# Weight sums of the block products: VectorE subtractions replaced by accumulating DMA transfers

## Chip, cores and metric

One core of one Trainium2 chip runs the whole program in one launch. The metric is device microseconds of one execution, the median of several runs; lower is better.

## What is computed

A trunk of two encoder layers on 512 tokens of width 1024, in float32, with a last RMSNorm. Each layer is

```python
x = x + 0.5 * swiglu(rmsnorm(x, ffn1_norm), ffn1_wg, ffn1_wu, ffn1_wd)
x = x + concat[neighbourhood attention, gated linear attention](rmsnorm(x, mix_norm)) @ w_out
x = x + 0.5 * swiglu(rmsnorm(x, ffn2_norm), ffn2_wg, ffn2_wu, ffn2_wd)

def swiglu(h, w_gate, w_up, w_down):
    return (jax.nn.silu(h @ w_gate) * (h @ w_up)) @ w_down
```

The change touches the gate and up projections (`h @ w_gate`, `h @ w_up`, 1024 by 2816) of the four feed-forward passes.

## The kernel before

Activations are held transposed, features in the partitions and tokens along the free axis, and all matrix products are made to float32 accuracy from a high and a low part: `split` makes the high part on ScalarE (ACT, line 149) and the remainder on VectorE (DVE, line 150), and `mm3` issues three matmuls (lines 176 to 178): high by high, high by low, low by high.

**Block products.** A pass has 11 column blocks of 256 for the gate and 11 for the up projection. The first three of each are computed directly (`direct_pairs`). The other eight pairs, 16 blocks a pass and 64 in all, go through `smat`, which replaces eight half-size partial products by seven, in the manner of Strassen and Winograd. Of the weights it takes four quarters a21, a11, a12, a22, each a 128 by 512 part of one tile `wraw`, loaded by one 1024 KB transfer on SyncE's queue (line 157), and four sums of them, s1 to s4. The activations' sums t1 to t4 are made once a pass in `prep_pair`. A partial product (`prod`) is 12 matmuls of 256 columns. In the order in which TensorE (PE) does them, the seven are: a12, a22, a11, s1, then s3 of the block before (`flush`, which runs the deferred `last`), then s2 and s4.

**Buffers.** `wraw` has two buffers, and the down projection's weights go through the same two. The split parts `wh` and `wl` have six each, for seven splits a block. So a split waits until a partial product ahead has given its buffer back, and the splits of one block run while TensorE still works on the block before. The four sums are tiles of their own (tag `ws`, five buffers), so `wraw` is free again once a12, a22 and a11 are split and the sums taken.

**Order.** Each engine works through a fixed list, written by the framework's scheduler, which lays the instructions out in time by its own estimates. An instruction that waits holds up all behind it in its engine's list. Between the feed-forward blocks lie the down projections: with `GROUPS = (4, 4, 3)` and three direct pairs, a pass has 3 block products, a down projection, 8 block products, a down projection, 5 block products, and the last down projection.

GpSimd (POOL) issues only the 32 loads of the attention bias (line 874).

Of the kernel before, what the change touches and what calls it, by code (L numbers as in the profile page):

```python
# [9 lines left out]
F32 = mybir.dt.float32  # L10
F32R = mybir.dt.float32r
U8 = mybir.dt.uint8
AF = mybir.ActivationFunctionType
ALU = mybir.AluOpType

P = 128
T = 512
H2 = T // 2
# [45 lines left out]
def trunk_kernel(ctx, tc, xin, wgu, wdn, win, wcode, wgate, wout, vec, rpbt,  # L64
                 lmask, onesid, out, depth=DEPTH, stop=None):
    nc = tc.nc
    V, S, G, PE = nc.vector, nc.scalar, nc.gpsimd, nc.tensor
# [18 lines left out]
    def gvec(stage, c):  # L86
        return vecs[:, stage * KD + c: stage * KD + c + 1]
# [12 lines left out]
    def nm(s):  # L100
        cnt[0] += 1
        return f"{st['lab']}_{s}_{cnt[0]}"

    def sl(name="s", dt=F32, tag="sl"):
        return sp.tile([P, T], dt, tag=tag, name=nm(name), bufs=TAGS[tag])
# [11 lines left out]
    def psum(tag):  # L117
        pool = {"mm": pm, "sc": ps2}.get(tag, ps1)
        return pool.tile([P, T], F32, tag=tag, name=nm(tag))
# [27 lines left out]
    def split(src, h, l, gain=None):  # L147
        if gain is None:
            S.activation(h, src, AF.Copy)  # L149
            V.tensor_tensor(l, src, h.bitcast(F32), op=ALU.subtract)  # L150
        else:
            S.activation(h, src, AF.Copy, scale=gain)
            V.scalar_tensor_tensor(l, src, gain, h.bitcast(F32), ALU.mult, ALU.subtract)

    def wload(src, n):
        raw = wp.tile([P, 2048], F32, tag="wraw", name=nm("wraw"))
        nc.sync.dma_start(raw[:, :n], src)
        return raw

    def wnew():  # L160
        return [wp.tile([P, T], F32R, tag=t, name=nm(t), bufs=6) for t in ("wh", "wl")]

    def wsplit(src, n=T):
        h, l = wnew()
        split(src, h[:, :n], l[:, :n])
        return h, l
# [8 lines left out]
    def mm3(ps, wh, wl, rh, rl, first, last, more=False):  # L175
        PE.matmul(ps, wh, rh, start=first, stop=False, skip_group_check=more)  # L176
        PE.matmul(ps, wh, rl, start=False, stop=False, skip_group_check=more)  # L177
        PE.matmul(ps, wl, rh, start=False, stop=last, skip_group_check=more)  # L178
# [6 lines left out]
    def prep_pair(i, stage):  # L185
        s = st["s"]
        ya, yb = sl("y"), sl("y")
        V.scalar_tensor_tensor(ya, xt[:, 2 * i, :], gvec(stage, 2 * i), s, ALU.mult, ALU.mult)
        V.scalar_tensor_tensor(yb, xt[:, 2 * i + 1, :], gvec(stage, 2 * i + 1), s, ALU.mult, ALU.mult)
        ta, tb = sl("y"), sl("y")  # L190
        b11, b12, b21, b22 = ya[:, :H2], ya[:, H2:], yb[:, :H2], yb[:, H2:]
        t1, t2, t3, t4 = ta[:, :H2], ta[:, H2:], tb[:, :H2], tb[:, H2:]
        V.tensor_tensor(t1, b12, b11, op=ALU.subtract)
        V.tensor_tensor(t2, b22, t1, op=ALU.subtract)
        V.tensor_tensor(t3, b22, b12, op=ALU.subtract)
        V.tensor_tensor(t4, b21, t2, op=ALU.subtract)
        tag = ("na", "na", "g0", "g1")[i]
        h0 = sl("xc", F32R, tag)
        split(b11, h0[:, :H2], h0[:, H2:])
        parts = [(h0[:, :H2], h0[:, H2:])]  # L200
        if i < 2:
            xg = gp_.tile([P, 4, T], F32R, tag="ga", name=nm("xc"))
        for j, src in enumerate((yb, ta, tb)):
            if i < 2 and j < 2:
                h, l = xg[:, 2 * j, :], xg[:, 2 * j + 1, :]
            else:
                h, l = sl("xc", F32R, tag), sl("xc", F32R, tag)
            split(src, h, l)
            parts += [(h[:, :H2], l[:, :H2]), (h[:, H2:], l[:, H2:])]
        XC[i] = dict(zip(("b11", "b21", "b22", "t1", "t2", "t3", "t4"), parts))  # L210
# [60 lines left out]
    def flush():  # L271
        while pend:
            pend.pop(0)()

    def wprep(src):
        raw = wload(src, 2048)
        a21, a11, a12, a22 = (raw[:, i * T:(i + 1) * T] for i in range(4))
        w12, w22, w11 = wsplit(a12), wsplit(a22), wsplit(a11)
        s1, s2, s3, s4 = (sl("ws", F32, "ws") for _ in range(4))
        V.tensor_tensor(s1, a21, a22, op=ALU.add)  # L280
        V.tensor_tensor(s2, s1, a11, op=ALU.subtract)
        V.tensor_tensor(s4, a12, s2, op=ALU.subtract)
        V.tensor_tensor(s3, a11, a21, op=ALU.subtract)
        return w12, w22, w11, wsplit(s1), s2, s4, s3

    def smat(src, post):
        w12, w22, w11, ws1, s2, s4, s3 = st.pop("pre", None) or wprep(src)
        o1, o2 = sl("o1"), sl("o2")

        def prod(ps, w, part, new=True):  # L290
            h, l = w
            for i in range(KP):
                c = slice(i * P, (i + 1) * P)
                mm3(ps, h[:, c], l[:, c], *XC[i][part], new and i == 0, i == KP - 1, not new)

        Y = psum("mm")
        Dp, Cp = Y[:, :H2], Y[:, H2:]
        prod(Dp, w12, "b21")
        yield
        prod(Cp, w22, "t4")  # L300
        S.activation(o1[:, :H2], Dp, AF.Copy)
        S.activation(o2[:, :H2], Cp, AF.Copy)
        yield
        A = psum("mm")[:, :H2]
        prod(A, w11, "b11")
        ws2, ws4, ws3 = wsplit(s2), wsplit(s4), wsplit(s3)
        V.tensor_tensor(o1[:, :H2], A, o1[:, :H2], op=ALU.add)
        yield
        B = psum("mm")[:, :H2]
        prod(B, ws1, "t1")  # L310
        S.activation(o2[:, H2:], B, AF.Copy)
        yield
        flush()
        yield
        prod(A, ws2, "t2", False)
        S.activation(o1[:, H2:], A, AF.Copy)
        yield
        prod(B, ws4, "b22", False)
        V.tensor_tensor(o1[:, H2:], B, o1[:, H2:], op=ALU.add)
        yield  # L320

        def last():
            prod(A, ws3, "t3", False)
            V.tensor_tensor(o2[:, H2:], A, o2[:, H2:], op=ALU.add)
            V.tensor_tensor(o2[:, :H2], A, o2[:, :H2], op=ALU.add)
            post(o1, o2)

        pend.append(last)

    def run(gen):  # L330
# [38 lines left out]
    def ffn(l, which):  # L369
# [9 lines left out]
        def gate_up(hid):  # L379
            n = fp[0]  # L380
            fp[0] += 1
            sg = []

            def post_g(o1, o2):
                for o in (o1, o2):
                    S.activation(o, o, AF.Silu)
                    sg.append(o)

            def post_u(o1, o2):
                for o, g in zip((o1, o2), sg):  # L390
                    V.tensor_tensor(o, o, g, op=ALU.mult)
                    add_hid(hid, o)

            yield from smat(wgu[idx, n, 0], post_g)
            yield from smat(wgu[idx, n, 1], post_u)

        def direct_pairs(hid):
# [25 lines left out]
            for i in range(3):  # L423
                prep_pair(i, stage)
            b11 = dmat(wgu[idx, 1, 1], ("tp", "o"))
            evac(b00, b01)
            prep_pair(3, stage)
            if NDF == 3:
                b20 = dmat(wgu[idx, 2, 0], ("mm", "mm"))
# [758 lines left out]
```

## Time and profile before

| | |
|---|---|
| median of 3 runs | 1929.98 us (1929.54 to 1930.05) |
| the profiled execution | 1929.63 us, of which the span is 1927.9 us |
| granted TensorE clock | 0.998 of full speed over the span |
| busy, share of the span | PE 99%, PEld 87%, DVE 73%, ACT 53%, POOL 1% |
| mean DMA rate | 97 GB/s |

PE is TensorE's matmuls, PEld its weight loads, which overlap them. Busy time is that of instructions at work, not of queues that wait. The span runs from the first to the last instruction; the time beside it holds what lies around them.

### The profile page before, as it was taken

The numbers are of one execution on the slowest core, as the hardware profiler recorded it, in microseconds if no ns is written. First come the engines' busy times: TensorE is split into PE (matmuls) and PEld (weight loads), VectorE is DVE, ScalarE is ACT, GpSimd is POOL, SyncE is SP. The second block draws the span as 40 slices with busy tenths as digits, with TensorE's granted clock in tenths as the row PEclk, the third lists the DMA queues.
The fourth block names the chain that finished last, engine by engine and source line by source line (L and its number), as shares of the span: only waits on it lengthen the run. The fifth ranks groups of instructions, "written<-read, shape, count | busy, mean of one in ns | idle before, by whom it ended". The sixth has DMA issues, their size and how long they took to land.

```text
span 1927.9 us, 32197 instructions
## 1 busy us (share of the span) xinstructions
PE 1912.1 (99%) x12490; PEld 1676.2 (87%) x12490; DVE 1412.6 (73%) x2705; ACT 1030.1 (53%) x1968; POOL 17.4 (1%) x36
## 2 busy tenths in 40 slices
PE   9999999999999999999999999999999999999997
PEld 8889989878788898989889899987887878999896
DVE  7958768677558976958787596776765688678585
ACT  6535536466665553635555264455666655446264
POOL 0000000000000000000000000000000000000000
PEclk9999999999999999999999999999999999999999
DMA  5332323322113322332323233232221133323322
GB/s 178 108 107 97 99 99 128 111 78 83 56 42 112 105 96 102 110 110 83 112 91 101 96 110 110 88 121 96 98 91 37 44 118 109 110 88 110 109 78 77
DMA packets 58249, 187.78 MB, mean 97 GB/s; under 512 B 6640, under 2 KB 13296, under 8 KB 45808
## 3 DMA queue, kind: packets, MB, share of 16 engines
q1 hardware_dynamic: 30480, 133.12, 20.3%
q10 hardware_dynamic: 25056, 44.22, 6.9%
q0 software_dynamic: 2560, 8.39, 1.3%
q8 instruction: 98, 1.61, 0.4%
q14 instruction: 55, 0.45, 0.1%
HBM read 183.60 MB, written 2.10 MB: 96 GB/s over the span
## 4 chain that ended last, share of the span: by engine, by line
PE 98%; DVE 1%; DMA 1%; ACT 0%; issue 0%; DVEq 0%; ACTq 0%
PE F_mm L176 14%; PE F_mm L178 14%; PE F_mm L177 14%; PE F_sc L176 9%; PE F_sc L177 9%; PE F_sc L178 9%; PE M_mm L176 6%; PE M_mm L178 6%; PE M_mm L177 6%; PE M_sc L171 2%; PE M_o L171 1%; PE M_mm L171 1%; PE M_tp L913 1%; PE M_mm L783 1%; DMA OP_wraw<-in_wout 0%; PE F_tp L176 0%
## 5 line engine op out<-in xcount | busy, mean ns | idle before, releaser
L149 ACT ACTIVATE F_wh<-F_wraw 128x512 fp32r<-128x512 f32 (+1 forms) x472 | 289.5, 617 | 449.5 <-PE F_sc L177 244.0
L176 PE MATMUL F_mm<-F_xc,F_wh 128*128 128x256 f32 x1792 | 500.9, 282 | 2.5 <-ACT F_wh L149 1.3
L177 PE MATMUL F_mm<-F_xc,F_wh 128*128 128x256 f32 x1792 | 501.6, 281 | 0.0
L178 PE MATMUL F_mm<-F_xc,F_wl 128*128 128x256 f32 x1792 | 495.3, 282 | 0.0
L150 DVE TENSOR_TENSOR F_wl<-F_wraw,F_wh 128x512 fp32r<-128x512 f32 (+1 forms) x472 | 312.3, 667 | 151.9 <-ACT F_wh L149 146.8
L176 PEld LDWEIGHTS F_mm<-F_xc,F_wh 128*128 128x128 f32 x1792 | 339.4, 190 | 5.1 <-ACT F_wh L149 1.9
L177 PEld LDWEIGHTS F_mm<-F_xc,F_wh 128*128 128x128 f32 x1792 | 340.3, 190 | 1.8
L178 PEld LDWEIGHTS F_mm<-F_xc,F_wl 128*128 128x128 f32 x1792 | 335.7, 190 | 0.0
L176 PE MATMUL F_sc<-F_hid,F_wh 128*128 128x512 f32 (+1 forms) x716 | 275.6, 387 | 1.3 <-DVE xt L471 1.3
L177 PE MATMUL F_sc<-F_hid,F_wh 128*128 128x512 f32 (+1 forms) x716 | 276.6, 386 | 0.0
L178 PE MATMUL F_sc<-F_hid,F_wl 128*128 128x512 f32 (+1 forms) x716 | 276.4, 386 | 0.0
L149 ACT ACTIVATE F_wh<-F_ws 128x512 fp32r<-128x512 f32 x256 | 162.0, 633 | 165.0 <-PE F_mm L177 104.8
L150 DVE TENSOR_TENSOR F_wl<-F_ws,F_wh 128x512 fp32r<-128x512 f32 x256 | 174.4, 687 | 40.0 <-ACT F_wh L149 36.9
L176 PEld LDWEIGHTS F_sc<-F_hid,F_wh 128*128 128x128 f32 x716 | 134.5, 188 | 29.0 <-DVE xt L471 3.0
L178 PEld LDWEIGHTS F_sc<-F_hid,F_wl 128*128 128x128 f32 x716 | 134.5, 188 | 26.5
L177 PEld LDWEIGHTS F_sc<-F_hid,F_wh 128*128 128x128 f32 x716 | 134.6, 188 | 25.8
L471 DVE SCALAR_TENSOR_TENSOR xt<-F_sc,xt 128x512 f32<-128x512 f32 x94 | 64.9, 691 | 96.1 <-PE F_sc L178 95.5
L176 PE MATMUL M_mm<-F_xd,M_wh 128*128 128x512 f32 x304 | 124.4, 409 | 0.0
L178 PE MATMUL M_mm<-F_xd,M_wl 128*128 128x512 f32 x304 | 119.6, 393 | 0.0
L177 PE MATMUL M_mm<-F_xd,M_wh 128*128 128x512 f32 x304 | 119.5, 393 | 0.0
L150 DVE TENSOR_TENSOR M_wl<-M_wraw,M_wh 128x512 fp32r<-128x512 f32 (+1 forms) x112 | 74.0, 667 | 47.2 <-ACT M_wh L149 31.9
L149 ACT ACTIVATE M_wh<-M_wraw 128x512 fp32r<-128x512 f32 (+1 forms) x112 | 67.6, 615 | 56.3 <-PE M_mm L177 32.8
(323 smaller groups left out, 3131.1 us busy)
## 6 DMA issues: line engine op xcount, KB each, us to landing
F_wraw<-in_wgu SPq DMA_DIRECT2D x64, 1024.0 KB, 4.7
F_wraw<-in_wdn SPq DMA_DIRECT2D x32, 1024.0 KB, 4.9
M_wraw<-in_win ACTq DMA_DIRECT2D x88, 256.0 KB, 3.6
F_wraw<-in_wgu ACTq DMA_DIRECT2D x76, 256.0 KB, 3.6
F_wraw<-in_wdn SPq DMA_DIRECT2D x16, 768.0 KB, 4.2
M_pp<-in_rpbt POOLq DMA_DIRECT2D x32, 256.0 KB, 3.1
M_wraw<-in_wout SPq DMA_DIRECT2D x16, 256.0 KB, 2.7
xt<-in_xin SPq DMA_DIRECT2D x8, 256.0 KB, 5.4
```

What stands on the lines that cost most here:

```text
L149: S.activation(h, src, AF.Copy)
L150: V.tensor_tensor(l, src, h.bitcast(F32), op=ALU.subtract)
L171: ins = PE.matmul(ps, lhs, rhs, **kw)
L176: PE.matmul(ps, wh, rh, start=first, stop=False, skip_group_check=more)
L177: PE.matmul(ps, wh, rl, start=False, stop=False, skip_group_check=more)
L178: PE.matmul(ps, wl, rh, start=False, stop=last, skip_group_check=more)
L471: V.scalar_tensor_tensor(xt[:, c, :], pss[j], 0.5, xt[:, c, :], ALU.mult, ALU.add)
L783: PE.matmul(dst, vs(2 * half + j), fa[:, o:o + P], start=False, stop=(j == 1))
L913: PE.transpose(pt[:, i * P:(i + 1) * P], pp[:, i * P:(i + 1) * P], idn)
```

## The change

The four sums are no longer made by VectorE in tiles of their own. After the load, accumulating transfers issued by GpSimd add weights from the source in HBM, or another quarter in SBUF, to the quarters in place: a21 becomes s1, a22 becomes s2, a11 becomes s3, a12 becomes s4. All are additions; the signs that this turns are made up for in `prep_pair`, in one evacuation (`scale=-1.0`) and in `last`. The quarters a12, a22 and a11 must be split before they are added to.

```diff
-        V.tensor_tensor(t1, b12, b11, op=ALU.subtract)
-        V.tensor_tensor(t2, b22, t1, op=ALU.subtract)
+        V.tensor_tensor(t1, b11, b12, op=ALU.subtract)
+        V.scalar_tensor_tensor(t2, t1, -1.0, b22, ALU.mult, ALU.subtract)
         V.tensor_tensor(t3, b22, b12, op=ALU.subtract)
-        V.tensor_tensor(t4, b21, t2, op=ALU.subtract)
+        V.tensor_tensor(t4, b21, t2, op=ALU.add)
...
+    def accumulate(dst, src):
+        nc.gpsimd.dma_start(dst, src, accum_op=ALU.add)
+
     def wprep(src):
         raw = wload(src, 2048)
         a21, a11, a12, a22 = (raw[:, i * T:(i + 1) * T] for i in range(4))
+        accumulate(a21, src[:, 3 * T:])
         w12, w22, w11 = wsplit(a12), wsplit(a22), wsplit(a11)
-        s1, s2, s3, s4 = (sl("ws", F32, "ws") for _ in range(4))
-        V.tensor_tensor(s1, a21, a22, op=ALU.add)
-        V.tensor_tensor(s2, s1, a11, op=ALU.subtract)
-        V.tensor_tensor(s4, a12, s2, op=ALU.subtract)
-        V.tensor_tensor(s3, a11, a21, op=ALU.subtract)
-        return w12, w22, w11, wsplit(s1), s2, s4, s3
+        accumulate(a22, src[:, :T])
+        accumulate(a22, src[:, T:2 * T])
+        accumulate(a11, src[:, :T])
+        accumulate(a12, a22)
+        return w12, w22, w11, wsplit(a21), a22, a12, a11
...
-        S.activation(o2[:, H2:], B, AF.Copy)
+        S.activation(o2[:, H2:], B, AF.Copy, scale=-1.0)
...
-            V.tensor_tensor(o2[:, H2:], A, o2[:, H2:], op=ALU.add)
-            V.tensor_tensor(o2[:, :H2], A, o2[:, :H2], op=ALU.add)
+            V.tensor_tensor(o2[:, H2:], o2[:, H2:], A, op=ALU.subtract)
+            V.tensor_tensor(o2[:, :H2], o2[:, :H2], A, op=ALU.subtract)
```

## Rows read from the trace of the kernel before

**Rows 1.** The page's first lines and its chain that ended last, by engine.

```profile
PE 1912.1 (99%) x12490; PEld 1676.2 (87%) x12490; DVE 1412.6 (73%) x2705; ACT 1030.1 (53%) x1968; POOL 17.4 (1%) x36
...
PE 98%; DVE 1%; DMA 1%; ACT 0%; issue 0%; DVEq 0%; ACTq 0%
```

**Rows 2.** A stretch of block products: length, engines' busy us (instructions), clock, DMA share, GB/s.

```profile
160.00:200.00 40.00, 40.00 (x339) 40.00 (x338) 37.46 (x69) 26.71 (x54) 0.00 (x0) 1.00 0.31 106
```

**Rows 3.** Groups by line and shape: busy us, mean ns, idle before.

```profile
L176 PE MATMUL F_mm<-F_xc,F_wh 128*128 128x256 f32 x1792 | 500.9, 282 | 2.5 <-ACT F_wh L149 1.3 <-ACT F_o L302 1.3
...
L282 DVE TENSOR_TENSOR F_ws<-F_wraw,F_ws 128x512 f32<-128x512 f32 x64 | 43.9, 686 | 0.8
...
L283 DVE TENSOR_TENSOR F_ws<-F_wraw 128x512 f32<-128x512 f32 x64 | 43.8, 684 | 0.3
```

**Rows 4.** ACT in order of time: start, us, instruction [idle before, releaser].

```profile
294.30 0.38 ACT L302 ACTIVATE F_o<-F_mm 128x256 f32<-128x256 f32 x1
294.93 0.63 ACT L149 ACTIVATE F_wh<-F_wraw 128x512 fp32r<-128x512 f32 x1 [0.25 <-ACT F_o L302]
296.36 0.63 ACT L149 ACTIVATE F_wh<-F_wraw 128x512 fp32r<-128x512 f32 x1 [0.80 <-PE F_mm L177]
...
297.74 0.64 ACT L149 ACTIVATE F_wh<-F_wraw 128x512 fp32r<-128x512 f32 x1 [0.47 <-PE F_mm L177]
299.40 0.63 ACT L149 ACTIVATE F_wh<-F_ws 128x512 fp32r<-128x512 f32 x1 [1.03 <-PE F_mm L177]
...
300.88 0.63 ACT L149 ACTIVATE F_wh<-F_ws 128x512 fp32r<-128x512 f32 x1
302.05 0.63 ACT L149 ACTIVATE F_wh<-F_ws 128x512 fp32r<-128x512 f32 x1 [0.54 <-PE F_mm L177]
302.67 0.63 ACT L149 ACTIVATE F_hid<-F_o 128x512 fp32r<-128x512 f32 x1
303.49 0.64 ACT L149 ACTIVATE F_wh<-F_ws 128x512 fp32r<-128x512 f32 x1 [0.19 <-PE F_mm L177]
304.03 0.36 ACT L301 ACTIVATE F_o<-F_mm 128x256 f32<-128x256 f32 x1
304.29 0.38 ACT L302 ACTIVATE F_o<-F_mm 128x256 f32<-128x256 f32 x1
304.92 0.63 ACT L149 ACTIVATE F_wh<-F_wraw 128x512 fp32r<-128x512 f32 x1 [0.25 <-ACT F_o L302]
306.35 0.63 ACT L149 ACTIVATE F_wh<-F_wraw 128x512 fp32r<-128x512 f32 x1 [0.80 <-PE F_mm L177]
```

**Rows 5.** DVE in order of time, the same stretch.

```profile
297.31 0.68 DVE L150 TENSOR_TENSOR F_wl<-F_wraw,F_wh 128x512 fp32r<-128x512 f32 x1
...
305.56 0.68 DVE L150 TENSOR_TENSOR F_wl<-F_ws,F_wh 128x512 fp32r<-128x512 f32 x1
...
311.00 0.43 DVE L319 TENSOR_TENSOR F_o<-F_mm,F_o 128x256 f32<-128x256 f32 x1 [0.25 <-PE F_mm L178]
```

**Rows 6.** DMA issues: transfer, issuing queue, count, KB each, median us from issue to landing.

```profile
F_wraw<-in_wgu SPq DMA_DIRECT2D x64, 1024.0 KB, 4.7
...
M_pp<-in_rpbt POOLq DMA_DIRECT2D x32, 256.0 KB, 3.1
M_wraw<-in_wout SPq DMA_DIRECT2D x16, 256.0 KB, 2.7
```

**Rows 7.** Line 874, GpSimd's loads: ns min/median/max on the engine; landing.

```profile
L874 POOL DMA_DIRECT2D M_pp<-in_rpbt x32: 536/536/670, 314.2 to 1439.2; - x32
...
DMA to landing us min/median/max: 2.9/3.1/5.7
```

**Rows 8.** DMA queues: packets, MB, share of the 16 engines' span.

```profile
q0 software_dynamic: 2560, 8.39, 1.3%
```

**Rows 9.** SyncE's queue: who waited for whom, us in total, times, longest.

```profile
SPq L157 <- DVE F_wl L150: 1119.4, 113, 16.6
```

## Prediction

> **What bounds the kernel now.** I read the page's busy shares and chain first: TensorE is at work for 1912.1 of 1927.9 us and holds 98% of the chain that ended last; VectorE, which the change relieves, holds 1% [rows 1]. Then a stretch of block products alone: TensorE 40.00 of 40 us, VectorE 37.46, GpSimd nothing [rows 2]. VectorE is nearly full there, yet TensorE never waits for it: before all 1792 leading matmuls of the block products TensorE sat idle for 2.5 us together [rows 3]. So a relief of VectorE has almost nothing to win, and what counts is whether the sums still arrive in time. For that I read ScalarE and VectorE instruction by instruction over one block [rows 4, 5], and last what GpSimd's transfers cost [rows 6 to 8].
>
> **The rhythm of a block.** The evacuation of line 302 comes once a block, at 294.30 and 304.29: a block lasts 9.99 us, one of its seven partial products 1.43 us. The seven splits of the block that TensorE reaches next run in this order: a12 at 294.93, a22 at 296.36, a11 at 297.74, s1 at 299.40, s2 at 300.88, s4 at 302.05, s3 at 303.49; the next block's a12 follows at 304.92 and its a22 at 306.35 [rows 4]. Those on raw weights wait for TensorE, that is for a buffer; they can't be pulled forward. a22's remainder is done on VectorE at 297.31 + 0.68 = 297.99. The product of s4 ends as line 319 adds it, at 311.00 [rows 5], so it began some 1.43 + 0.28 us (one matmul's length, rows 3) earlier, at 309.3.
>
> **What it removes.** 4 x 64 subtractions and additions on VectorE at 0.68 us, 175 us of its time [rows 3], 2.7 us a block. None of it is on TensorE's path: its worth is at most the 2.5 us above.
>
> **What costs nothing.** The activation sums in `prep_pair` keep their count, size and engine, as do the evacuation with a scale and the two operations of `last`. One of them becomes a two-step operation of the same shape; it is made once a pass, beside the direct products, and its cover is the same as before.
>
> **What it adds.** Five transfers of 256 KB a block, 320 in all, on GpSimd's queue. GpSimd gives 0.54 us to an issue of that size [rows 7]: 2.7 us of each 10, on an engine that is idle, so hidden even at twice that. In DMA time, 32 such loads took 1.3% of the engines [rows 8]; 320 take ten times that, 13%, and 26% if adding doubles the traffic, beside the 0.31 of now [rows 2]. Bandwidth is no bound.
>
> Latency is. The sum s2 needs two transfers into a22, one after the other, and s4 a third that reads the finished a22. All three come after a22's split, since that needs the untouched quarter. So where VectorE took 0.68 us a step, there are now three trips in a row between the split of a22 and the split of s4. Between them lie in GpSimd's list the transfer into a11, which holds up nothing (a11 is split by then), and, ahead, the one into a21, which needs only the load.
>
> **One trip.** No accumulating transfer is in this trace. The nearest row is GpSimd's plain load of the same 256 KB: 3.1 us, 2.9 at best [rows 6, 7]. An accumulating one must read the destination too. 768 KB more cost 4.7 - 2.7 = 2.0 us on SyncE's queue, 0.67 us per 256 KB [rows 6]: 3.8 us. The 1024 KB load of each block streams for some 4 x 0.67 = 2.7 us of the 10; a trip that meets it loses about its own streaming time of 1.3 us, a quarter of the time: 0.3. I take 4.1 us, nearer the single load, since the fixed part is most of it and is paid once. The bounds are 2.9 (adding is free) and 6.2 (two transfers end to end).
>
> The Trainium skill has a fit for this path ("DMA: Bandwidth & Descriptors", section "Anatomy of one DMA — SWDGE (gpsimd) path"): about 2.0 us and the bytes at 436 GB/s, here 2.6 us a transfer. By it three trips are an estimated 7.8 us, which the 10.0 us below would hide, and the time would stay near 1930 us. This trace's 3.1 us for the same bytes speaks against it.
>
> **The room.** s4's split takes 0.63 on ScalarE and 0.68 on VectorE, so it must start by 309.3 - 1.3 = 308.0; a22 is free at 298.0. Three trips have 10.0 us, 3.3 us each. At 4.1 they miss it by 2.3 us.
>
> **What is late next.** ScalarE's list has the split of s4 ahead of the next block's split of a22 (302.05 against 306.35). If that order stands, the waiting s4 holds that a22 up, and a22 starts the next three trips: a closed loop. Its period is three trips, the split of s4 on ScalarE (0.63), that of a22 (0.63) and its remainder on VectorE (0.68): 3 x 4.1 + 1.94 = 14.24 us a block, against 9.99: 4.25 us more. All else that ScalarE does between the two can be done in the waiting time, if the list puts it there. If it stays between them as now (0.63 + 0.64 + 0.36 + 0.38 + 0.63 = 2.64 us, rows 4), the period is 16.88, 6.89 more.
>
> The 64 blocks run in 12 unbroken rows of 3, 8 and 5 a pass; the first of a row has its transfers under way beside a down projection and should not pay: 52 pay. The sum is 52 x 4.25 = 221 us on the profiled execution's 1929.6 (0.35 under the median): 2151 us. With the looser list 52 x 6.89 = 358: 2288.
>
> `wraw` is also held longer: its last reader becomes the split of s3, done at 305.56 + 0.68, not a split of raw weights as now, after which SyncE issues the next load [rows 9]. Held from issue (4.7), through the two splits of a12 and a22 (about 2), three trips (12.3) and the splits of s4 and s3 (about 2), a buffer is taken for 21 us; two of them allow a block each 10.5 us, less than the loop asks for. No cost of its own.
>
> **The rivals.**
> 1. The list is laid out anew so that ScalarE never stands in front of a missing sum. Then only TensorE's own order binds: from the end of s1's product by a22's split (296.36 to 297.99, 1.63), three trips, s4's split (1.31), and five products (s4, a12, a22, a11, s1; 7.14) to the end of the s1 product two blocks on. Two blocks take 10.08 + 3 x 4.1, one 11.19: 52 x 1.20 = 62 us, 1992 us. For it: the order is remade by a scheduler that knows of these transfers. Against it: its estimates must be near the truth.
> 2. No slower: a trip takes at most 3.3 us, so that the same loop gives (10.08 + 9.9)/2 = 9.99 and ScalarE stays ahead of TensorE. For it: the plain load's 2.9 to 3.1. Against it: a destination that must be read, and the list. It gives 1927 to 1930 us. The deciding point is 3.3 us a trip. The Trainium skill's fit ("DMA: Bandwidth & Descriptors", the same section) would lead here.
> 3. Faster: the free VectorE closes TensorE's gaps. All of TensorE's idle time is 15.8 us [rows 1], 2.5 of it in these products; 3.9 us would be needed to be seen.
> 4. Adding is slower than two transfers: over 6.2 us a trip the loop exceeds 20.54 us a block, 52 x 10.55 = 549 us and more, over 2478 us. Nothing in the rows shows how fast a DMA engine adds.
>
> **How the numbers follow.** The kept order with 2.9 to 6.2 us a trip: 0.58 (10.64 to 20.54 us a block, 1963 to 2478 us). Rival 1: 0.22 (with 6.2 us a trip 14.34 a block, 2156). Rival 4: 0.08. Rival 2: 0.09. Rival 3: 0.03. A difference of 0.2%, 3.9 us, is about what a measurement of this kernel tells from no change. So slower 0.88, same 0.09, faster 0.03. The range leaves out rivals 2 to 4, 0.20: from 1940, a rival 1 with a trip of about 3.45 us (0.22 x 52 = 12), to 2480. The prediction is 2151.
>
> **What the changed profile would show.** Line 157's loads as before and 320 GpSimd issues, with a landing of about 4 us; VectorE's busy time near 1412.6 - 175 = 1237 us; TensorE idle before lines 176 of the s2 and s4 products, released by ScalarE's split; ScalarE idle before splits of `F_wraw`, released by a DMA; the largest gap once a block, at 14 us from block to block. Wrong would be: a landing of 3 us with TensorE still at 40 of 40 (rival 2), ScalarE idle little and blocks of 11 us (rival 1), or a trip of 7 us and more (rival 4).

## The result, and the profile after

The changed kernel takes 2318.78 us (median of 4 runs, 2314.96 to 2327.32) against 1929.81 us for the kernel before on the same chip (4 runs, 1929.54 to 1930.05): 1.2022 times as long, 95% interval 1.1988 to 1.2056. That is 389 us, 6.1 us for each of the 64 block products. The prediction, 2151 us, had the direction and the kind of loss; the loss was 1.76 times the 221 us it worked out, and lies 31 us above its case of the looser list, 2288 us. The profiled execution took 2320.2 us, with a span of 2318.3.

The page of the changed kernel: busy time, chain that ended last, the two queues that carry the block products' weights, the costliest groups, and the DMA issues. They answer to [rows 1, 3, 6, 8].

```profile
PE 2097.9 (90%) x12490; PEld 1808.1 (78%) x12490; DVE 1255.2 (54%) x2449; ACT 1012.0 (44%) x1968; POOL 296.0 (13%) x356
...
q0 software_dynamic: 48640, 92.30, 22.8%
q1 hardware_dynamic: 30480, 133.12, 16.9%
...
PE 52%; DMA 28%; issue 10%; DVE 4%; POOL 3%; ACT 2%; POOLq 0%; DVEq 0%; ACTq 0%
...
L176 PE MATMUL F_mm<-F_xc,F_wh 128*128 128x256 f32 x1792 | 570.0, 321 | 191.7 <-ACT F_wh L149 189.1
...
F_wraw<-in_wgu SPq DMA_DIRECT2D x64, 1024.0 KB, 4.9
F_wraw<-in_wgu POOLq DMA_DIRECT2D x256, 256.0 KB, 4.8
...
F_wraw<-F_wraw POOLq DMA_DIRECT2D x64, 256.0 KB, 3.3
```

Transfers, 1% of the chain before, hold 28% of it. VectorE fell from 1412.6 to 1255.2 us, near the 1237 expected, and nothing came of that. TensorE's idle time grew from 15.8 to 220.4 us, 191.7 us of it in front of line 176, the first matmul on a freshly split weight, and what ended 189.1 us of that was ScalarE's split. The same 12490 matmuls also show 185.8 us more busy time; the granted clock over the span was 0.926, against 0.998 before. Nearly all of this lies in the block products' own matmuls: their three lines of 1792 take 1683.1 us against 1497.8, while the 692 large matmuls of line 176 in the down projections take 394 ns each against 390.

The same stretch as in [rows 2], same columns:

```profile
160.00:200.00 40.00, 33.80 (x236) 31.66 (x234) 15.54 (x29) 13.58 (x29) 9.57 (x11) 0.91 0.62 130
```

TensorE, VectorE and ScalarE are all less busy than before, TensorE does 236 matmuls where it did 339, GpSimd is busy for 9.57 of the 40 us, and the DMA engines are at 0.62 of their time. So a latency, not an engine's work, sets the pace. The chain that ended last says the same of 160 to 230 us (shares of this stretch; pieces reach over its ends, so they sum to more than 100%):

```profile
by line: DMA F_wraw<-in_wgu 50.0%; issue 23.6%; DMA F_wraw<-F_wraw 20.5%; DVE F_wl L150 7.6%; POOL F_wraw L278 4.9%; ACT F_wh L149 3.6%; DVE F_o L312 0.3%; DVEq L150 0.2%; POOLq L278 0.2%; ACTq L149 0.1%
```

No matmul of TensorE is in it, so its lower clock does not set the pace of these blocks. In two of its blocks the chain goes by the next tile's load (187.91 to 192.58, 207.60 to 212.65) in place of the first addition into a22: the load waits until the split of s3 frees the tile, and the addition into the next a21, which waits for the load, stands in GpSimd's list ahead of the second one into a22. Both ways end at nearly the same time: the issue for a21 ends 0.14 and 0.28 us before the second addition goes out. What ScalarE and TensorE waited for, from the table of waits (total, times, longest):

```profile
ACT F_wh L149 <- DMA F_wraw<-in_wgu: 198.0, 66, 6.6
...
PE F_mm L176 <- ACT F_wh L149: 189.1, 121, 3.9
...
ACT F_wh L149 <- DMA F_wraw<-F_wraw: 151.5, 62, 4.2
```

66 and 62 waits, for 64 blocks: about once a block ScalarE stands before the split of s2 for a transfer from HBM, and once before that of s4 for the transfer from the finished a22. One block, first GpSimd, then ScalarE, then VectorE, in order of time:

```profile
189.99 1.76 POOL L278 DMA_DIRECT2D F_wraw<-in_wgu  x2 [6.49 <-DVE F_wl L150]
193.14 1.87 POOL L278 DMA_DIRECT2D F_wraw<-in_wgu  x2 [1.39 <-DMA F_wraw<-in_wgu]
201.03 0.86 POOL L278 DMA_DIRECT2D F_wraw<-F_wraw  x1 [6.02 <-DMA F_wraw<-in_wgu]
209.07 1.75 POOL L278 DMA_DIRECT2D F_wraw<-in_wgu  x2 [7.18 <-DVE F_wl L150]
```

```profile
195.54 0.38 ACT L307 ACTIVATE F_o<-F_mm 128x256 f32<-128x256 f32 x1
...
200.82 0.63 ACT L149 ACTIVATE F_wh<-F_wraw 128x512 fp32r<-128x512 f32 x1 [2.56 <-DMA F_wraw<-in_wgu]
205.61 2.71 ACT L149 ACTIVATE F_wh<-F_wraw 128x512 fp32r<-128x512 f32 x5 [4.16 <-DMA F_wraw<-F_wraw]
...
214.35 0.38 ACT L307 ACTIVATE F_o<-F_mm 128x256 f32<-128x256 f32 x1
```

```profile
206.28 3.10 DVE L150 TENSOR_TENSOR F_wl<-F_wraw,F_wh 128x512 fp32r<-128x512 f32 x5 [4.10 <-ACT F_wh L149]
```

The closed loop of the prediction is there to read. At 189.99 a22 is split, and the first addition into it goes out. The second, the last of the two issues at 193.14 (the other adds to the next block's a21), goes out at 194.14, 0.29 us after the first is in. At 200.74 that is in: ScalarE splits s2, and 0.29 us later the addition of a22 into a12 starts. It is in at 205.6, and then ScalarE does five splits in one go: s4, s3, and the next block's a12, a22 and a11, which had stood behind s4 all this time. The next a22 is free at 208.8, and at 209.07 its first addition goes out. From 189.99 to 209.07 are 19.08 us: 4.15 + 6.89 + 4.54 for the three trips, with the gaps to the next issue, and 3.5 from the last landing to the next first trip. Line 307, once a block, comes at 195.54 and 214.35, 18.81 us apart; before it was 9.99 us.

This block is one of the slower ones. Of the 48 loops that the trace shows from one block's first addition into a22 to the next's, one lasts 17.54 us in the mean: 13.06 us for the three trips and 4.48 us for what stands between them.

The time between those evacuations, over the whole kernel, says where the 389 us lie. 40 of the 52 intervals inside the 12 rows of blocks last 17.4 us in the mean (13.8 to 20.1) against 10.0: 293 us. The first interval of each row is shorter than before, 87 us against 102 in all: -15. The 11 stretches from one row to the next grew by 107 us. Together 385, the rest lies at the ends.

### The profile page after: what moved, and what is told of

It reads as the page before. It is cut to its first block, busy times and chain, and to the rows that moved or that the text cites. A ratio compares the mean times of both kernels' runs of the same rounds, so it can differ in the third digit from the quotient of the medians.

```text
span 2318.3 us, 32591 instructions
## 1 busy us (share of the span) xinstructions
PE 2097.9 (90%) x12490; PEld 1808.1 (78%) x12490; DVE 1255.2 (54%) x2449; ACT 1012.0 (44%) x1968; POOL 296.0 (13%) x356
## 3 DMA queue, kind: packets, MB, share of 16 engines
q0 software_dynamic: 48640, 92.30, 22.8%
q1 hardware_dynamic: 30480, 133.12, 16.9%
## 4 chain that ended last, share of the span: by engine, by line
PE 52%; DMA 28%; issue 10%; DVE 4%; POOL 3%; ACT 2%; POOLq 0%; DVEq 0%; ACTq 0%
DMA F_wraw<-in_wgu 20%; DMA F_wraw<-F_wraw 8%; PE F_sc L176 6%; PE F_sc L177 6%; PE F_sc L178 6%; PE M_mm L176 5%; PE M_mm L178 5%; PE M_mm L177 5%; DVE F_wl L150 3%; PE F_mm L176 3%; PE F_mm L178 3%; PE F_mm L177 3%; POOL F_wraw L278 3%; ACT F_wh L149 2%; PE M_sc L171 2%
## 5 line engine op out<-in xcount | busy, mean ns | idle before, releaser
L150 DVE TENSOR_TENSOR F_wl<-F_wraw,F_wh 128x512 fp32r<-128x512 f32 (+1 forms) x728 | 467.8, 676 | 518.1 <-ACT F_wh L149 512.4
L176 PE MATMUL F_mm<-F_xc,F_wh 128*128 128x256 f32 x1792 | 570.0, 321 | 191.7 <-ACT F_wh L149 189.1
L149 ACT ACTIVATE F_wh<-F_wraw 128x512 fp32r<-128x512 f32 (+1 forms) x728 | 419.2, 614 | 718.6 <-PE F_sc L177 252.1
L178 PE MATMUL F_mm<-F_xc,F_wl 128*128 128x256 f32 x1792 | 559.0, 318 | 14.8 <-DVE F_wl L150 14.3
L176 PEld LDWEIGHTS F_mm<-F_xc,F_wh 128*128 128x128 f32 x1792 | 393.4, 220 | 222.8 <-ACT F_wh L149 218.4
L177 PE MATMUL F_mm<-F_xc,F_wh 128*128 128x256 f32 x1792 | 554.1, 311 | 0.0
L178 PEld LDWEIGHTS F_mm<-F_xc,F_wl 128*128 128x128 f32 x1792 | 387.4, 219 | 38.5 <-DVE F_wl L150 38.2
L278 POOL DMA_DIRECT2D F_wraw<-in_wgu x256 | 224.0, 933 | 1374.9 <-DVE F_wl L150 806.1
L177 PEld LDWEIGHTS F_mm<-F_xc,F_wh 128*128 128x128 f32 x1792 | 396.9, 221 | 0.9
L312 DVE TENSOR_TENSOR F_o<-F_mm,F_o 128x256 f32<-128x256 f32 x64 | 27.0, 423 | 129.6 <-PE F_mm L178 129.6
```

The source lines that it names most:

```text
L278: nc.gpsimd.dma_start(dst, src, accum_op=ALU.add)
```

## The experiments

Each times one edit of the changed kernel; times are medians, the ratio is against the kernel before (1929.6 to 1929.9 us in these runs).

**Plain copies.** The transfers overwrite and do not add, so the four sums are left out; their number, sizes and order stay.

```diff
-        nc.gpsimd.dma_start(dst, src, accum_op=ALU.add)
+        nc.gpsimd.dma_start(dst, src)
```

> All five transfers stay where they are, with the same sources, sizes, waits and order, but copy instead of adding, so the sums are left out. Theory (three trips in a row close a loop with the order of the splits): only the length of a trip changes. If adding makes up most of the 1.7 us by which these trips (4.8 us) exceed GpSimd's plain loads in the kernel before (3.1 us), three trips become 3 to 4 us shorter a block, 64 x 3.5 = 220 us: 2060 to 2140 us. If the excess is contention among the transfers, it stays and the time is over 2250 us. Rival (the DMA engines can't move five adding transfers a block): much the same gain as the first, since a plain copy moves half the bytes; this run sizes the price of adding and does not part the two.

2113.37 us (1.0935 to 1.0968). Its issues and its queue:

```profile
q0 software_dynamic: 28160, 92.30, 12.1%
...
F_wraw<-in_wgu POOLq DMA_DIRECT2D x256, 256.0 KB, 3.3
...
F_wraw<-F_wraw POOLq DMA_DIRECT2D x64, 256.0 KB, 2.3
```

Adding costs 205 of the 389 us; with plain copies in the same chain the other 184 stay. A loop of 3.3 + 3.3 + 2.3 us and the 4.1 us that stood between the landings and the issues above gives 13.0 us a block; measured, the 40 intervals inside the rows last 13.4 us in the mean. So the loop explains the plain copies too.

**One trip fewer.** The last link of the chain, s4, goes back to VectorE.

```diff
-        accumulate(a12, a22)
+        V.tensor_tensor(a12, a12, a22, op=ALU.add)
```

> s4 = a12 + s2 goes back to VectorE, in place; the other four transfers stay. Theory (three trips in a row): the third trip, 3.3 us from issue to landing with 0.3 us ahead of it, becomes a 0.7 us instruction: 2.9 us a block less, 64 x 2.9 = 186 us: 2110 to 2160 us. Rival (capacity of the DMA engines or of GpSimd): one of five transfers less, a fifth of the 389 us: about 2240 us.

2170.29 us (1.1232 to 1.1278): 149 us back, just outside what the theory gave and far from the 2240 of the rival. A trip of 3.3 us replaced by some 0.7 us on VectorE, 64 times, is 166 us.

**The addition outside the chain.** s1 goes back to VectorE; the three trips stay.

```diff
-        accumulate(a21, src[:, 3 * T:])
+        V.tensor_tensor(a21, a21, a22, op=ALU.add)
```

> s1 = a21 + a22 goes back to VectorE, in place; the other four transfers stay, the three in a row among them. Theory: the transfer into a21 is not in the row of three, but in GpSimd's list it stands between the two into a22, where it waits for the next load, and it streams beside the second; without it the second issue comes up to 1 us sooner and its trip is up to 1.5 us shorter: 0.5 to 2 us a block, 2190 to 2290 us. Rival (capacity): one of five transfers less, about 2240 us as in the run with s4 on VectorE, and so the same time as that one (2170 us) or near it.

2258.84 us (1.1691 to 1.1723): 60 us back, 0.9 us a block. With four transfers left, as many as in the run before, this one is 89 us slower: which transfer goes decides, not how many there are. Even the transfer that no sum of the chain needs lengthens the loop: it stands in GpSimd's list between the two additions into a22, and moves its data beside them. The second is what counts: followed as above, the three trips of a loop take 11.87 us here in place of 13.06, and what stands between them 4.45 against 4.48.

**A third buffer for the tile.** `wraw` gets three buffers (`ws`, which the sums no longer need, goes from five to two and gives the room).

```diff
-        raw = wp.tile([P, 2048], F32, tag="wraw", name=nm("wraw"))
+        raw = wp.tile([P, 2048], F32, tag="wraw", name=nm("wraw"), bufs=3)
...
```

> The changed kernel with three buffers of the weight tile in place of two (the tag of the old sums goes from five buffers to two to make room; only the attention stage uses it now). Theory (three trips behind the split of a22, closed into a loop by the order of the splits): the loop holds no buffer wait, so little changes: 2230 to 2320 us. Rival (the weight tile is held too long for two buffers, which is what was left in the two runs before that shortened or shifted the trips): a tile is held some 23 us, three buffers allow a block each 7.7 us, so most of the loss goes: 1930 to 2050 us.

2307.47 us (1.1934 to 1.1967). That is 11 us back. The rival, that the longer hold of the tile is what binds by itself, falls. The buffer does not take all waiting for a load away: GpSimd still waits for one, now of the block after next, ahead of the second addition into a22 (194.4 us in 39 waits, 281.7 in 45 with two buffers). The run before, without the addition into a21, has no such wait in GpSimd's list, and its loss is still 329 us.

**Breaking the chain at a22.** A fifth quarter c, loaded on SyncE's queue, takes the sum s2, so that its additions need not wait for a22's split. The transfers on GpSimd stay five, all adding, beside the extra load; the count in the expectation is wrong in this. The tile grows by a quarter, and `ws` goes to three buffers.

```diff
...
+        nc.sync.dma_start(c, src[:, :T])
+        accumulate(c, src[:, 3 * T:])
         accumulate(a21, src[:, 3 * T:])
+        accumulate(c, src[:, T:2 * T])
...
-        accumulate(a22, src[:, :T])
-        accumulate(a22, src[:, T:2 * T])
         accumulate(a11, src[:, :T])
-        accumulate(a12, a22)
+        accumulate(a12, c)
...
```

> s2 is built in a fifth quarter of the weight tile, loaded a second time with a21, so its two additions need only the load and no longer wait for the split of a22. Seven transfers a block where the change has five, six of them adding. Theory (three trips in a row behind the split): one trip is left behind a split, the loop is 3.3 us for it and 3.3 us for the splits, less than TensorE's 10 us: 1930 to 2010 us. Rival (capacity): more transfers, so no faster than 2319 us, by the count 1930 + 389 x 7/5 = 2475 us. Second rival (the weight tile is held too long for two buffers): it is held as long or longer, so 2319 us or more.

2159.72 us (1.1171 to 1.1208). With more data moved it is 159 us faster than the changed kernel, as the chain would have it, but the expected time is missed by 150 us. From 160 to 230 us (columns as in [rows 2]) the DMA engines are busy 0.77 of the time, and TensorE still waits:

```profile
160.00:230.00 70.00, 57.25 (x424) 56.02 (x423) 33.47 (x60) 29.08 (x61) 20.34 (x24) 0.88 0.77 177
```

**Splits ahead.** The program asks for the next block's splits of a12, a22, a11 and s1 before this block's s2, s4 and s3, so that ScalarE's list no longer closes the loop. This is done between neighbouring blocks, not across a down projection.

```diff
         prod(A, w11, "b11")
+        if nxt is not None:
+            st["pre"] = wprep(nxt)
         ws2, ws4, ws3 = wsplit(s2), wsplit(s4), wsplit(s3)
...
```

> The same five transfers, but the next block's load, its transfers and its splits of a12, a22, a11 and s1 come ahead of this block's splits of s2, s4 and s3 in the program (within a pair and between pairs, not across a down projection). Theory: the next block's trips start before this block's sums are needed, the three trips get two blocks' time, so a block takes (14 + 3.3)/2 = 8.7 us by that loop, below TensorE's own; with TensorE's loop of the prediction (10.08 + 14)/2 = 12.0: 1930 to 2060 us. Rival (capacity): the same transfers in the same number, about 2319 us. Second rival (weight tile held too long): 2319 us or more, since two blocks now hold both buffers at once for longer.

2186.41 us (1.1266 to 1.1362), 132 us back. And with the third buffer as well:

```diff
+            st["pre"] = wprep(nxt)
...
+        raw = wp.tile([P, 2048], F32, tag="wraw", name=nm("wraw"), bufs=3)
...
```

> The splits of the next block ahead of this block's splits of the sums, and three buffers of the weight tile. Theory (two loops, the trips and the hold of the tile, either of which alone is enough to slow a block): the order gives the trips two blocks' time, 8.7 us a block, and the third buffer 7.7 us a block, both below TensorE's 10: 1930 to 2000 us. Rival (capacity of the DMA engines or of GpSimd's queue for five adding transfers a block): no faster than with the order alone, 2170 to 2190 us.

2156.36 us (1.1158 to 1.1188), 162 us back. Both missed their numbers. The reason stands in GpSimd's timeline of the second:

```profile
182.51 0.87 POOL L278 DMA_DIRECT2D F_wraw<-F_wraw  x1 [7.24 <-DMA F_wraw<-in_wgu]
183.05 3.01 POOL L278 DMA_DIRECT2D F_wraw<-in_wgu  x3
188.60 0.87 POOL L278 DMA_DIRECT2D F_wraw<-in_wgu  x1 [2.54 <-DMA F_wraw<-in_wgu]
197.62 0.87 POOL L278 DMA_DIRECT2D F_wraw<-F_wraw  x1 [8.15 <-DMA F_wraw<-in_wgu]
198.15 3.01 POOL L278 DMA_DIRECT2D F_wraw<-in_wgu  x3
```

ScalarE's list no longer closes the loop, GpSimd's does: the addition into a12 waits at its head for the second one into a22, and the next block's first addition stands behind it. From 182.51 to 197.62 are two trips in a row, 15.1 us.

**GpSimd's list reordered**, on top of the last kernel: the planner must keep the transfers in the program's order, and a block's addition into a12 comes after the next block's first one into a22.

```diff
         accumulate(a22, src[:, :T])
-        accumulate(a22, src[:, T:2 * T])
+        for f in st.pop("held", ()):
+            accumulate(*f)
         accumulate(a11, src[:, :T])
-        accumulate(a12, a22)
+        accumulate(a22, src[:, T:2 * T])
+        st["held"] = [(a12, a22)]
...
```

> The run with the splits ahead and three buffers, and GpSimd's list written out: the third transfer of a block (into a12) stands behind the first of the next block, so that no next block's first transfer waits behind it. Theory (what was left in that run is GpSimd's list: the third transfer waits at its head for the second to land, and the next block's two trips start only then, two trips of 5 and 9 us a block in a row): the two trips of neighbouring blocks overlap, and a block takes 10 to 12 us: 1940 to 2060 us. Rival (capacity of the DMA engines for five adding transfers a block, whose trips were as long as 9 us there): no better than that run, 2156 us.

2070.71 us (1.0712 to 1.0756): 86 us back, 11 us outside the theory's range. The stretch from 160 to 230 us shows what comes up next; the DMA engines are busy 0.90 of it:

```profile
160.00:230.00 70.00, 63.93 (x496) 63.07 (x495) 41.76 (x75) 35.86 (x76) 24.80 (x29) 0.93 0.90 189
```

**Two sums without a chain.** s1 and s3 by transfers, s2 and s4 on VectorE: neither transfer waits for the other.

```diff
-        accumulate(a22, src[:, :T])
-        accumulate(a22, src[:, T:2 * T])
+        s2, s4 = sl("ws", F32, "ws"), sl("ws", F32, "ws")
+        V.tensor_tensor(s2, a21, a11, op=ALU.add)
+        V.tensor_tensor(s4, a12, s2, op=ALU.add)
         accumulate(a11, src[:, :T])
-        accumulate(a12, a22)
-        return w12, w22, w11, wsplit(a21), a22, a12, a11
+        return w12, w22, w11, wsplit(a21), s2, s4, a11
```

> Only s1 (a21 += a22) and s3 (a11 += a21) are made by adding transfers, with the turned signs; s2 = s1 + a11 and s4 = a12 + s2 are made on VectorE in tiles of their own, as before the change. Two transfers a block, neither behind the other, and VectorE still relieved of 88 us. Theory: no trips in a row; s1's trip needs only the load, s3's only the split of a11 and the sum s2, and s3 is needed last. The weight tile is held some 5 + 5 + 2 + 5 + 2 us, under 20, so two buffers suffice or nearly: 1928 to 1960 us. Rival (capacity): two fifths of the 389 us: 2085 us.

1965.64 us (1.0173 to 1.0201). Two transfers a block still cost 36 us. The waits point to VectorE's list, which blocks in its turn:

```profile
DVE F_ws L286 <- DMA F_wraw<-in_wgu: 169.6, 62, 7.1
...
PE F_mm L176 <- DVE F_o L312: 19.0, 21, 2.5
```

VectorE stands before s2 until s1 has landed, and an evacuation behind it keeps TensorE, for 19.0 of the 36 us. No run takes this wait out by itself.

**Five transfers, none in a chain.** The kernel above plus three adding transfers a block whose results nothing reads, one into a22 after its split and two into spare tiles.

```diff
         accumulate(a11, src[:, :T])
+        accumulate(a22, src[:, :T])
+        for d in st["dum"]:
+            accumulate(d, a12)
...
```

> The run with s1 and s3 alone by adding transfers, with three more of the same size added to each block that nothing waits for: one adds to a22 after its split, two add a12 to spare tiles. Five adding transfers a block as in the change, none behind another's landing. Theory (the loss is in trips that wait for trips): close to the run without them, 1965 us, and longer by what contention adds to s1's trip: 1965 to 2040 us. Rival (capacity for five adding transfers a block): 2150 us or more, as in the runs with five.

2010.27 us (1.0411 to 1.0448): as many adding transfers as the change has, for 80 us instead of 389. (Two of these five read SBUF and three HBM; in the change it is one and four.) But they fill the DMA engines, 0.92 of the same stretch:

```profile
160.00:230.00 70.00, 62.39 (x510) 60.91 (x509) 48.55 (x89) 36.89 (x77) 25.66 (x30) 1.00 0.92 198
```

**One sum.** Only s3 by a transfer; it is needed last.

```diff
-        accumulate(a21, src[:, 3 * T:])
...
-        accumulate(a22, src[:, :T])
-        accumulate(a22, src[:, T:2 * T])
+        s1, s2, s4 = (sl("ws", F32, "ws") for _ in range(3))
+        V.tensor_tensor(s1, a21, a22, op=ALU.add)
+        V.tensor_tensor(s2, s1, a11, op=ALU.add)
+        V.tensor_tensor(s4, a12, s2, op=ALU.add)
         accumulate(a11, src[:, :T])
-        accumulate(a12, a22)
...
```

> Only s3 (a11 += a21) by an adding transfer, s1, s2 and s4 on VectorE in tiles of their own; signs as in the change. VectorE is relieved of 44 us, and the one transfer has several us to spare. Theory: TensorE is never late and has nothing to win from VectorE: 1928 to 1933 us. Rival (a free VectorE is worth something to TensorE): under 1926 us. If a transfer at the head of GpSimd's list or a longer held weight tile cost by themselves: over 1934 us.

1929.97 us (0.9991 to 1.0009), the time of the kernel before. Its busy times and the landing of its one transfer a block:

```profile
PE 1911.9 (99%) x12490; PEld 1675.7 (87%) x12490; DVE 1371.5 (71%) x2641; ACT 1021.2 (53%) x1968; POOL 73.1 (4%) x100
...
F_wraw<-in_wgu POOLq DMA_DIRECT2D x64, 256.0 KB, 3.7
```

VectorE is relieved of 41 us, TensorE's time is the same. No version here beats the kernel before.

## Why the prediction was right in kind and short in size

**Right: a relief of VectorE is worth nothing.** With s3 alone moved, VectorE lost 41 us and the kernel gained none.

**Right: three trips in a row, closed into a loop by ScalarE's list.** The timeline shows it step by step, and the runs part it from its rivals. Taking one trip out gave 149 us back. Taking ScalarE's list out gave 132, and with the third buffer 162, though that buffer alone gave 11. The same number of adding transfers outside a chain cost 80 us and not 389. That the list would be laid out anew (rival 1) did not happen: ScalarE still stood in front of s4, 62 times. Nor did a trip short enough to hide (rival 2): even plain copies, 3.0 us a trip in the mean, lost 184 us. The prediction's deciding point for rival 2, 3.3 us a trip, belongs to the loop of rival 1; by its own kept order a trip had to be under (9.99 - 1.94)/3 = 2.7 us. Adding slower than two transfers (rival 4) was not the case in the median.

**Mis-sized by a little: the trip.** The term was 4.1 us. Measured, an adding transfer of 256 KB from HBM takes 4.8 us in the median and one from SBUF 3.3, which come to 12.9 for three and not 12.3; over the 48 loops the three take 13.06 us in the mean. The term for one trip with nothing beside it, 3.8 us, was close: where s3 alone is moved, the transfer lands after 3.7. Too small was the 0.3 us for what it meets: the second into a22 shares the DMA engines with the transfers into a21 and a11 and in the block shown took 6.6 us, the three 15.0, the longest but one of the 48. The Trainium skill's fit for this path ("DMA: Bandwidth & Descriptors", section "Anatomy of one DMA — SWDGE (gpsimd) path"), 2.6 us by my estimate, is short of the plain copies from HBM, 3.3 us, and by more of the adding ones, 4.8; the measurement decides.

**Mis-sized by more: what stands between the trips.** I took 1.94 us, with all other work of ScalarE put into the waiting time; the looser list had 4.58. Over the 48 loops it was 4.48 in the mean, in the block shown 4.1: ScalarE's list kept s3 and the next a12 between s4 and the next a22, and each landing costs GpSimd another 0.29 us before the next issue. Together: 13.06 + 4.48 = 17.54 us against 14.24; of the 3.3 us more, 0.8 are the trips' and 2.5 stand between them. Also the sentence that a21's transfer lies "ahead" failed: without it the kernel took 60 us less. That a11's "holds up nothing" was not tried by itself.

**Mis-counted: the blocks that pay.** I let 52 pay. The first interval of a row is indeed no longer than before, but its last block pays beside the down projection: the stretches between rows grew by 107 us in 11 places, which the sum put at nothing. The lower clock gives little of it outside the blocks: the large matmuls of the down projections, 394 ns against 390, are 5.4 us longer in all. The rest of the 107 us was not followed block by block.

**Too easily said: "Bandwidth is no bound."** I put the 320 transfers at 13 to 26% of the DMA engines; their queue took 22.8% of the longer span, 529 us; less the 25 us of the 32 bias loads [rows 8], 504/320 = 1.57 us of each engine's time for one. The plain copies, with a span of 2114.6 us, took (12.1% of it - 25)/320 = 0.72. Five additions, and the load at 16.9% of 2318.3 us x 1.049/133.12 MB = 3.1 us, make 10.9 us a block, more than the 9.99 that TensorE needs. It is hidden behind the loop's 17.4, but it is the next bound: with the loop open the DMA engines stood at 0.90 and 0.92. It can explain up to the 80 us of the five transfers apart, of which 36 were there with two.

**Left open.** What holds the kernel with the fifth quarter at 2160 us was not parted among GpSimd's list, the hold of the tile and the DMA engines. The clock's share was not measured by itself; in the stretch of [rows 2] it was 0.91 where TensorE waits and 1.00 before, and TensorE's products are not in the chain of the blocks.

## What to carry to other kernels

Moving work from a busy engine to transfers pays only if that engine is waited for; look first at what idles in front of it. In-place sums by transfers turn steps of 0.7 us into trips of 3 to 7 us, one behind the other, and every engine's fixed list that has a consumer of the chain ahead of its next producer closes it into a loop: price the period of that loop, with all that stands between, against the rhythm of the kernel. Open one list and look at the next (here ScalarE's, then GpSimd's, then VectorE's), and sum the DMA engines' time per block, counting an addition as two copies.

## What the runs showed of the hardware

An adding transfer of 256 KB took 1.57 us of the DMA engines' time against 0.72 for a plain one, landed after 4.8 us against 3.3 from HBM and 3.3 against 2.3 from SBUF, and cost GpSimd 0.86 us an issue against 0.54. So adding costs some 2.2 times the transfer time, but in these two kernels only 1.0 to 1.5 us of latency, and more of the issuing engine. Part of that latency is the other transfers': one adding transfer a block, in the kernel with s3 alone, landed after 3.7 us.
